# Layer 0's first products in three weight chunks and four accumulators, with x transposed between them

## The chip, the cores and the metric

The kernel runs on one core of a Trainium2 chip. The metric is the device time of one execution in microseconds (us), the median of several runs. The engines are TensorE (PE in the profile; its weight loads are PEld), VectorE (DVE), ScalarE (ACT), GpSimd (POOL) and SyncE (SP), which here issues the weight transfers.

## The reference, cut to what matters

Two post-norm transformer layers over 512 tokens of width 1024. Each layer attends to its own tokens and, with four heads, to a memory of 256 rows, and then runs a SwiGLU (a mixture of experts in layer 1). The change touches the first lines of layer 0: the memory's keys and values, and what stands right behind them.

```
kvm = mem @ w_mem_kv[i]                 # (256, 1024) @ (1024, 512)
km = kvm[..., :hm]; vm = kvm[..., hm:]  # hm = 256: keys, values
proj = x @ w_in_swa[j]                  # (512, 1024) @ (1024, 1408): q, k, v, qc
q, k = partial_rope(q, cos, sin), partial_rope(k, cos, sin)
```

## The kernel before, in words

Every product is made of three fp16 matmuls (`mm3`, lines 238 to 240): high by high, high by low and low by high. Weights arrive in f32 as chunks of at most 2096 columns per partition. Each chunk is loaded by one DMA on SP's queue (line 123) into one of three `raw` buffers. ACT then writes its high part (`wh<-raw`, line 150) and DVE its low part (`wl<-raw`, line 159), in pieces of `W.piece` columns, 1048 unless it is set otherwise. `W.tick(n)` puts n such steps into the program where it is called: one new ACT piece, and one DVE piece of those that are waiting, as long as more than `LAG = 1` wait. `W.need(i)` forces all pieces up to chunk i; a use of a weight calls it. A fourth load can only be issued when the first chunk has been converted.

The order on each engine is the order in which the program is written; nothing is moved later. At the start (lines 699 to 761) this order is:

1. SP loads the memory's 256 rows (two DMAs), the two chunks of `w_mem_kv[0]`, the four tiles of x, and then, as buffers come free, `w_in_swa`.
2. PE transposes the memory (line 742). ACT and DVE copy it out as `memTh` and `memTl`.
3. Four steps follow: keys of heads 0 and 1, keys of heads 2 and 3, values of the first 128 rows, values of the last 128. Each is 24 matmuls over all of K in one PSUM bank of 256 columns (8 blocks of 128 rows of K, three matmuls each). Behind each step stand its copies out of PSUM (`k_evac` is four ACT and two DVE instructions, a value tile one and one), then `W.tick(2)`, which converts a chunk of `w_in_swa`, then the 8 transposes of one tile of x (`transposed`, line 391) with two ACT and two DVE copies, `xTh` and `xTl`.
4. DVE works out the angles of the rotary embedding from the positions (lines 752 to 760, 24 small instructions), ACT the sine and cosine.
5. `v_proj(t)` for the four tiles of x: 24 matmuls of 192 columns each, with the first unit of `w_in_swa` (`u_a`, two chunks of 4 blocks of K, 448 columns a block, converted in pieces of 1048 and 744 columns). The query projections and the attention of layer 0 follow.

PSUM has four single banks (`bank()`) and two tiles of two banks (`bank2()`), each group used in turn.

Of the kernel before, what the change touches and what calls it, by code (L numbers as in the profile page):

```python
# [19 lines left out]
NT = S // 128  # L20
KD = D // 128
# [5 lines left out]
ML = 256  # L27
# [17 lines left out]
SQ = 8.0  # L45
SV = 8.0
SP = 4096.0
SG = 32768.0
DS = 1.0 / (SX * SW)
# [3 lines left out]
PIECE = 1048  # L53
# [157 lines left out]
def trunk_kernel(ctx, tc, x, mem, positions, w_in_swa, attn_sinks, w_in_fox, b_forget, w_mem_kv, w_out,  # L211
# [13 lines left out]
    def bank(name="A"):  # L225
        return ps.tile([128, 512], FT, name="bk", tag="A", bufs=4)

    def bank2():
        return ps.tile([128, 2, 512], FT, name="bk2", tag="S", bufs=2)

    def high(o, i, scale=1.0):
        nc.scalar.activation(o, i, AF.Copy, scale=scale)  # L232

    def low(o, i, scale, h):
        nc.vector.scalar_tensor_tensor(o, i, scale, h, op0=OP.mult, op1=OP.subtract)  # L235

    def mm3(o, lh, ll, rh, rl, first, last, **kw):
        nc.tensor.matmul(o, lh, rh, start=first, stop=False, **kw)  # L238
        nc.tensor.matmul(o, lh, rl, start=False, stop=False, **kw)  # L239
        nc.tensor.matmul(o, ll, rh, start=False, stop=last, **kw)  # L240
# [5 lines left out]
    W = Weights(nc, rawp, hlp)  # L246

    def wsrc(w):
        return w.rearrange("(k p) c -> p k c", p=128)

    def add_cols(w, c0, c1):
        v = wsrc(w)
        return W.add((v[:, 0:4, c0:c1], 4 * (c1 - c0)), (v[:, 4:8, c0:c1], 4 * (c1 - c0)))
# [11 lines left out]
    def unit(u, n):  # L265
        return [View(W, u, i, n) for i in range(2)]

    u_m0 = add_cols(w_mem_kv[0], 0, 512)
    u_a = add_cols(w_in_swa[0], 960, 1408)
    u_k = add_cols(w_in_swa[0], 512, 960)  # L270
    u_q = add_cols(w_in_swa[0], 0, 512)
# [56 lines left out]
    xtok = base.tile([128, NT, D], FT, name="xtok")  # L328
    xT = (xTp.tile([128, KD, S], FH, name="xTh"), xTp.tile([128, KD, S], FH, name="xTl"))
    memT = (memp.tile([128, KD, ML], FH, name="memTh"), memp.tile([128, KD, ML], FH, name="memTl"))  # L330
# [54 lines left out]
    def transposed(src, dst, t, before=lambda q: None):  # L385
        for q in range(2):
            before(q)
            b = bank()
            bv = b.rearrange("p (k n) -> p k n", n=128)
            for k in range(4):  # L390
                nc.tensor.transpose(bv[:, k, :], src[:, (4 * q + k) * 128:(4 * q + k + 1) * 128], identf)
            o = (slice(None), slice(4 * q, 4 * q + 4), slice(t * 128, (t + 1) * 128))
            high(dst[0][o], bv, SX)
            low(dst[1][o], bv, SX, dst[0][o])

    def halves(half):
        return slice(64 * half, 64 * half + 64), slice(64 - 64 * half, 128 - 64 * half)
# [13 lines left out]
    def k_evac(KH, KL, heads, src, sc, cols):  # L411

        for half in range(2):
            for r in halves(half):
                high(KH[r, heads(half), cols], src(half), sc)
        for half in range(2):
            a = halves(half)[0]
            low(KL[a], src(half), sc, KH[a, heads(half), cols])
# [199 lines left out]
    def mem_kv(u, memT, KM, VM):  # L618
        def kpair(p):
            wh, wl = unit(u, 512)  # L620
            b = bank()[:, :ML]
            c = slice(p * 128, p * 128 + 128)
            for k in range(KD):
                mm3(b, wh[:, k, c], wl[:, k, c], memT[0][:, k, :], memT[1][:, k, :], k == 0, k == KD - 1)
            k_evac(KM[0], KM[1][:, p, :], lambda hf: 2 * p + hf, lambda hf: b[64 * hf:64 * hf + 64, :], DS * SQ,
                   slice(0, ML))

        def vtile(m):
            wh, wl = unit(u, 512)
            b = bank()[:, :ML]  # L630
            c = slice(m * 128, m * 128 + 128)
            for k in range(KD):
                mm3(b, memT[0][:, k, c], memT[1][:, k, c], wh[:, k, 256:], wl[:, k, 256:], k == 0, k == KD - 1)
            high(VM[0][:, m, :], b, DS * SV)
            low(VM[1][:, m, :], b, DS * SV, VM[0][:, m, :])
            if m == 1:
                W.free(u)

        return [lambda: kpair(0), lambda: kpair(1), lambda: vtile(0), lambda: vtile(1)]
# [55 lines left out]
    def mem_tiles(pool):  # L695
        return ((pool.tile([128, MH, ML], FH, name="KMh"), pool.tile([128, MH // 2, ML], FH, name="KMl")),
                (pool.tile([128, 2, ML], FH, name="VMh"), pool.tile([128, 2, ML], FH, name="VMl")))

    KM0, VM0 = mem_tiles(sp)
    memtok = [sp.tile([128, D], FT, name="P", bufs=3) for _ in range(2)]  # L700
    mr = mem[0].rearrange("(t p) d -> p t d", p=128)
    for t in range(2):
        nc.sync.dma_start(memtok[t], mr[:, t, :])
    W.load_n(2)
    for t in range(NT):
        nc.sync.dma_start(xtok[:, t, :], xr[:, t, :])
    W.load()
# [30 lines left out]
    for t in range(2):  # L738
        for q in range(2):
            b = bank().rearrange("p (k n) -> p k n", n=128)  # L740
# [2 lines left out]
            o = (slice(None), slice(4 * q, 4 * q + 4), slice(t * 128, (t + 1) * 128))  # L743
            high(memT[0][o], b, SX)
            low(memT[1][o], b, SX, memT[0][o])
    m0 = mem_kv(u_m0, memT, KM0, VM0)
    for i, f in enumerate(m0):
        f()
        W.tick(2)
        transposed(xtok[:, i, :], xT, i)  # L750

    nc.vector.tensor_copy(posf, pos)
    for j in range(8):
# [155 lines left out]
    for i, u in enumerate(u_fi):  # L909
        wh, wl = unit(u, 256)  # L910
        if i == 0:
            bb = [bank2(), bank2()]
            for t in range(NT):
                if t == NT - 1:
                    transposed(xtok[:, t, :], xT, t)
                c = slice(t * 128, t * 128 + 128)
                for jj in range(2):
                    f = slice(jj * 128, jj * 128 + 128)
# [7 lines left out]
        else:  # L926
            for jj in range(2):
                f = slice(jj * 128, jj * 128 + 128)
                b = bank2()
# [18 lines left out]
    for h in range(2):  # L948
# [6 lines left out]
        for gi, u in enumerate(u_fo[h]):  # L955
            kn = (8, 8, 6)[gi]
            wh, wl = unit(u, 512)
            for t in range(NT):
                c = slice(t * 128, t * 128 + 128)
# [29 lines left out]
    wh, wl = unit(u_xv2, 524)  # L989
    for t in range(NT):  # L990
        c = slice(t * 128, t * 128 + 128)
        b = bank()
# [294 lines left out]
    def fetch(pool, oh, n, rows_too=True):  # L1287

        b = bank()
        idx = pool.tile([128, 2], I32, name="idx", bufs=2)  # L1290
        to = pool.tile([128, 2], I32, name="to", bufs=2)
        rows = []
        for r, m in n:
            i = r // 128
            for t in range(NT):
                nc.tensor.matmul(b[:m, 2 * i:2 * i + 2], oh[:, t, r:r + m], tid[:, t, :], start=t == 0,
                                 stop=t == NT - 1)
        for r, m in n:
            i = r // 128
            if not rows_too:  # L1300
                break
            nc.vector.tensor_copy(idx[:m, i:i + 1], b[:m, 2 * i:2 * i + 1])
            g = pool.tile([128, D], FT, name=f"xg{i}")
            nc.gpsimd.indirect_dma_start(out=g[:m, :], out_offset=None, in_=x2d,
                                         in_offset=bass.IndirectOffsetOnAxis(ap=idx[:m, i:i + 1], axis=0))
            rows.append(g)
        sums_at(pool, b, n, to)
        return rows, b, idx, to
# [262 lines left out]
    with tc.For_i(0, nit) as _:  # L1571
# [35 lines left out]
        rows, b, _, to = fetch(lp, oh, n)  # L1607
# [153 lines left out]
    for s in range(NEXP):  # L1761
        C = CAP[s]
        act = [mx.tile([128, KF, CMAX], FH, name=f"act{i}", bufs=1) for i in range(2)]
        for i, u in enumerate(u_ei[s]):
            if i < 2 * QUADS:
                if i % 2 == 0:
                    sa = mx.tile([128, 4, CMAX], FT, name="sa", bufs=2)
                b = bank2()
# [82 lines left out]
```

## Time and profile before

| | |
|---|---|
| median of 3 runs | 1679.88 us (1676.76 to 1680.16) |
| the profiled execution: its own time | 1677.88 us |
| its span in the profile | 1676.1 us |
| PE busy | 1616.5 us, 96% |
| DVE busy | 1225.9 us, 73% |
| ACT busy | 981.9 us, 59% |
| mean granted clock of TensorE | 0.984 |

The span is the time from the first to the last instruction of the profiled execution; 1.78 us lie around it. Matmuls are pipelined, so a busy PE is not a PE at its peak: the step from the start of one matmul to the start of the next tells how fast they run.

### The profile page before, as it was taken

How to read it: one execution, taken by the hardware profiler on the slowest of the kernel's cores; microseconds unless marked ns; L12 is line 12 of the kernel's file. 1: busy time of each engine (PE TensorE's matmuls, PEld its weight loads, DVE VectorE, ACT ScalarE, POOL GpSimd, SP SyncE). 2: the span in 40 equal slices, each digit the busy share in tenths (PEclk: the TensorE clock that was granted, in tenths of full speed). 3: DMA queues.
4: the chain of work that ended last, by engine and by line, in shares of the span. 5: the costliest groups of instructions: out<-in, count | busy, mean ns of one | idle time of the engine just before them, and what ended most of it. 6: DMA issues, size and time to landing. Idle time of an engine off the chain costs nothing.

```text
span 1676.1 us, 42682 instructions
## 1 busy us (share of the span) xinstructions
PE 1616.5 (96%) x18407; PEld 1278.2 (76%) x18407; DVE 1225.9 (73%) x1814; ACT 981.9 (59%) x1507; POOL 283.7 (17%) x280
## 2 busy tenths in 40 slices
PE   7999999999999799999799999999999999999996
PEld 6775564444444647665599999999999999999993
DVE  6788644333532658787799698996979979699997
ACT  5676333322212457665287687776877778665773
POOL 0342200000100400003130031201303031130250
PEclk8999999999999899999899999999999999999998
DMA  7511033322632132110499899999999999999993
GB/s 264 177 52 51 1 126 126 100 101 88 206 100 69 61 126 84 33 61 16 170 378 326 308 376 393 370 340 318 384 367 365 365 321 371 343 287 371 351 369 117
DMA packets 180531, 370.13 MB, mean 221 GB/s; under 512 B 6573, under 2 KB 49581, under 8 KB 180336
## 3 DMA queue, kind: packets, MB, share of 16 engines
q1 hardware_dynamic: 173264, 343.48, 57.4%
q0 software_dynamic: 4768, 15.47, 3.9%
q10 hardware_dynamic: 2304, 8.39, 1.3%
q8 instruction: 146, 2.39, 0.6%
q14 instruction: 49, 0.40, 0.1%
HBM read 355.08 MB, written 12.39 MB: 219 GB/s over the span
## 4 chain that ended last, share of the span: by engine, by line
PE 39%; issue 3%; DVE 3%; ACT 2%; DMA 2%; POOL 2%; ACTq 0%; POOLq 0%; DVEq 0%
PE bk L1387 8%; PE bk L1389 8%; PE bk L1388 8%; PE bk L1416 4%; PE bk L1417 4%; PE bk L1418 4%; DVE wl L159 2%; ACT wh L150 1%; DMA raw<-in_w_exp_in_dram 1%; POOL act L1405 1%; PE bk L238 1%; PE bk L239 1%; PE bk L240 1%; POOL expert_sums L1320 1%; PE bk L1437 1%
## 5 line engine op out<-in xcount | busy, mean ns | idle before, releaser
L159 DVE SCALAR_TENSOR_TENSOR wl<-raw,wh 128x1048 f16<-128x1048 f32 (+3 forms) x654 | 794.4, 1265 | 104.4 <-ACT wh L150 104.1
L150 ACT ACTIVATE wh<-raw 128x1048 f16<-128x1048 f32 (+3 forms) x654 | 641.1, 1041 | 102.5 <-PE bk L240 49.6
L1387 PE MATMUL bk<-xa,wh 128*128 128x160 f16 (+3 forms) x1280 | 261.3, 232 | 5.7 <-DVE eid L1538 5.7
L1388 PE MATMUL bk<-xa,wh 128*128 128x160 f16 (+3 forms) x1280 | 261.2, 232 | 0.0
L1389 PE MATMUL bk<-xa,wl 128*128 128x160 f16 (+3 forms) x1280 | 261.1, 232 | 0.0
L1387 PEld LDWEIGHTS <-wh 128*128 128x128 f16 x2560 | 250.8, 98 | 6.5 <-issue 5.8
L1388 PEld LDWEIGHTS <-wh 128*128 128x128 f16 x2560 | 250.8, 98 | 2.7 <-issue 2.4
L1389 PEld LDWEIGHTS <-wl 128*128 128x128 f16 x2560 | 250.8, 98 | 0.0
L1418 PE MATMUL bk<-act,wl 128*128 128x160 f16 (+6 forms) x1232 | 235.3, 227 | 1.4 <-DVE wl L159 1.4
L1417 PE MATMUL bk<-act,wh 128*128 128x160 f16 (+6 forms) x1232 | 235.3, 227 | 0.0
L1416 PE MATMUL bk<-act,wh 128*128 128x160 f16 (+6 forms) x1232 | 235.3, 227 | 0.0
L1387 PE MATMUL bk<-xe,wh 128*128 128x128 f16 (+2 forms) x1280 | 223.2, 221 | 2.1 <-DVE sa L1403 1.4
L1388 PE MATMUL bk<-xe,wh 128*128 128x128 f16 (+2 forms) x1280 | 223.1, 221 | 0.0
L1389 PE MATMUL bk<-xe,wl 128*128 128x128 f16 (+2 forms) x1280 | 223.1, 221 | 0.0
L238 PE MATMUL bk<-xTh,wh 128*128 128x512 f16 (+2 forms) x656 | 205.7, 324 | 4.9 <-DVE KLx L235 4.0
L239 PE MATMUL bk<-xTl,wh 128*128 128x512 f16 (+2 forms) x656 | 205.5, 323 | 0.5 <-DVE xTl L235 0.5
L240 PE MATMUL bk<-xTh,wl 128*128 128x512 f16 (+2 forms) x656 | 205.5, 323 | 0.0
L1405 POOL TENSOR_TENSOR act<-sa,act 128x512 f16<-128x512 f32 (+6 forms) x40 | 106.8, 2671 | 280.7 <-ACT act L232 280.7
L238 PEld LDWEIGHTS <-wh 128*128 128x128 f16 x944 | 92.8, 98 | 55.3 <-DVE KLx L235 4.4
L240 PEld LDWEIGHTS <-wl 128*128 128x128 f16 x944 | 92.8, 98 | 48.6 <-DVE wl L159 1.6
L239 PEld LDWEIGHTS <-wh 128*128 128x128 f16 x944 | 92.9, 98 | 47.3 <-issue 1.6
L1418 PEld LDWEIGHTS <-wl 128*128 128x128 f16 x1232 | 120.5, 98 | 1.8 <-DVE wl L159 1.8
(349 smaller groups left out, 2787.4 us busy)
## 6 DMA issues: line engine op xcount, KB each, us to landing
raw<-in_w_exp_in_dram SPq DMA_DIRECT2D x176, 1024.0 KB, 9.0
raw<-in_w_exp_out_dram SPq DMA_DIRECT2D x85, 1024.0 KB, 9.3
raw<-in_w_ffn_in_dram SPq DMA_DIRECT2D x22, 1024.0 KB, 5.2
raw<-in_w_out_dram SPq DMA_DIRECT2D x8, 1024.0 KB, 5.0
raw<-in_w_ffn_out_dram SPq DMA_DIRECT2D x8, 1024.0 KB, 5.6
raw<-in_w_in_fox_dram SPq DMA_DIRECT2D x8, 1024.0 KB, 5.2
raw<-in_w_mem_kv_dram SPq DMA_DIRECT2D x4, 1024.0 KB, 7.1
raw<-in_w_in_swa_dram SPq DMA_DIRECT2D x4, 896.0 KB, 8.9
```

The lines of the kernel that those rows point to most:

```text
L150: self.nc.scalar.activation(h[:, p:e], t[:, p:e], AF.Copy, scale=SW)
L159: self.nc.vector.scalar_tensor_tensor(l, src, SW, h, op0=OP.mult, op1=OP.subtract)
L238: nc.tensor.matmul(o, lh, rh, start=first, stop=False, **kw)
L239: nc.tensor.matmul(o, lh, rl, start=False, stop=False, **kw)
L240: nc.tensor.matmul(o, ll, rh, start=False, stop=last, **kw)
L1387: nc.tensor.matmul(o, wh[:, k, c], xe[0][:, k, :C], start=first, stop=False, skip_group_check=True)
L1388: nc.tensor.matmul(o, wh[:, k, c], xe[1][:, k, :C], start=False, stop=False, skip_group_check=True)
L1389: nc.tensor.matmul(o, wl[:, k, c], xe[0][:, k, :C], start=False, stop=k == KD - 1, skip_group_check=True)
L1405: lambda: nc.gpsimd.tensor_sub(act[1][:, j, :C], sa[:, :, :C], act[0][:, j, :C])]
L1416: nc.tensor.matmul(o, wh[:, k, c], act[0][:, kk, :C], start=first, stop=False, skip_group_check=True)
L1417: nc.tensor.matmul(o, wh[:, k, c], act[1][:, kk, :C], start=False, stop=False, skip_group_check=True)
L1418: nc.tensor.matmul(o, wl[:, k, c], act[0][:, kk, :C], start=False, stop=kk == KF - 1, skip_group_check=True)
```

## The change

`w_mem_kv[0]` becomes three chunks of 2, 2 and 4 blocks of K in place of two of 4 and 4. All three are loaded ahead of x, which takes all three `raw` buffers. While they are converted, `W.piece` is 512. The four results (keys of two head pairs, values of two tiles) get an accumulator each, in two tiles of two banks, `kb` and `vb`. Chunk one is multiplied into all four, then chunk two, then comes the first tile of x to transpose, and then chunk three, one result at a time, each followed by its copies and the next tile of x. The conversions of `w_in_swa` that stood between the steps now stand behind all of them, as `W.tick(4)`.

```
--- before.py
+++ after.py
@@ -265,7 +265,8 @@
     def unit(u, n):
         return [View(W, u, i, n) for i in range(2)]
 
-    u_m0 = add_cols(w_mem_kv[0], 0, 512)
+    wm = wsrc(w_mem_kv[0])
+    u_m0 = W.add(*[(wm[:, a:b, :], 512 * (b - a)) for a, b in ((0, 2), (2, 4), (4, 8))])
     u_a = add_cols(w_in_swa[0], 960, 1408)
     u_k = add_cols(w_in_swa[0], 512, 960)
     u_q = add_cols(w_in_swa[0], 0, 512)
@@ -701,7 +702,7 @@
     mr = mem[0].rearrange("(t p) d -> p t d", p=128)
     for t in range(2):
         nc.sync.dma_start(memtok[t], mr[:, t, :])
-    W.load_n(2)
+    W.load_n(3)
     for t in range(NT):
         nc.sync.dma_start(xtok[:, t, :], xr[:, t, :])
     W.load()
@@ -743,11 +744,39 @@
             o = (slice(None), slice(4 * q, 4 * q + 4), slice(t * 128, (t + 1) * 128))
             high(memT[0][o], b, SX)
             low(memT[1][o], b, SX, memT[0][o])
-    m0 = mem_kv(u_m0, memT, KM0, VM0)
-    for i, f in enumerate(m0):
-        f()
-        W.tick(2)
-        transposed(xtok[:, i, :], xT, i)
+    W.piece = 512
+    kb, vb = bank2(), bank2()
+
+    def m0_part(u, ks, ps_):
+
+        wh, wl = unit(u, 512)
+        for p in ps_:
+            for k in ks:
+                if p < 2:
+                    c = slice(p * 128, p * 128 + 128)
+                    mm3(kb[:, p, :ML], wh[:, k, c], wl[:, k, c], memT[0][:, k, :], memT[1][:, k, :], k == 0, k == KD - 1)
+                else:
+                    c = slice((p - 2) * 128, (p - 2) * 128 + 128)
+                    mm3(vb[:, p - 2, :ML], memT[0][:, k, c], memT[1][:, k, c], wh[:, k, 256:], wl[:, k, 256:],
+                        k == 0, k == KD - 1)
+
+    for ks in ((0, 1), (2, 3)):
+        m0_part(u_m0, ks, range(4))
+    W.need(W.first[u_m0 + 1] - 1)
+    transposed(xtok[:, 0, :], xT, 0)
+    for p in range(4):
+        m0_part(u_m0, range(4, KD), [p])
+        if p < 2:
+            k_evac(KM0[0], KM0[1][:, p, :], lambda hf, p=p: 2 * p + hf, lambda hf, p=p: kb[64 * hf:64 * hf + 64, p, :ML],
+                   DS * SQ, slice(0, ML))
+        else:
+            high(VM0[0][:, p - 2, :], vb[:, p - 2, :ML], DS * SV)
+            low(VM0[1][:, p - 2, :], vb[:, p - 2, :ML], DS * SV, VM0[0][:, p - 2, :])
+        if p < NT - 1:
+            transposed(xtok[:, p + 1, :], xT, p + 1)
+    W.free(u_m0)
+    W.piece = PIECE
+    W.tick(4)
 
     nc.vector.tensor_copy(posf, pos)
     for j in range(8):
```

The first place where instructions move is DVE's queue around the angles. `xTl` are the copies of x, `KMl` and `VMl` those of keys and values, line 159 is a piece of weights, and the rows from `posf` (a cast) to the last `n_132` are the angles. Before, the queue goes:

```order
L159 SCALAR_TENSOR_TENSOR wl<-raw,wh 128x744
L159 SCALAR_TENSOR_TENSOR wl<-raw,wh 128x1048
L235 SCALAR_TENSOR_TENSOR xTl<-bk,xTh 128x4x128 x2
L235 SCALAR_TENSOR_TENSOR VMl<-bk,VMh 128x256
L159 SCALAR_TENSOR_TENSOR wl<-raw,wh 128x744
L159 SCALAR_TENSOR_TENSOR wl<-raw,wh 128x1048
L235 SCALAR_TENSOR_TENSOR xTl<-bk,xTh 128x4x128 x2
L752 CAST posf<-pos 128x4
```

Of the change, the same queue up to the angles, and then the end of the angles:

```order
L235 SCALAR_TENSOR_TENSOR xTl<-bk,xTh 128x4x128 x2
L235 SCALAR_TENSOR_TENSOR VMl<-bk,VMh 128x256
L235 SCALAR_TENSOR_TENSOR xTl<-bk,xTh 128x4x128 x2
L235 SCALAR_TENSOR_TENSOR VMl<-bk_168,VMh 128x256
L159 SCALAR_TENSOR_TENSOR wl<-raw,wh 128x1048
L159 SCALAR_TENSOR_TENSOR wl<-raw,wh 128x744
L159 SCALAR_TENSOR_TENSOR wl<-raw,wh 128x1048
L781 CAST posf<-pos 128x4
```

```order
L730 SCALAR_TENSOR_TENSOR ang<-n_132,ang 128x32 x3
L786 TENSOR_SCALAR ang<-ang 128x32
L788 SCALAR_TENSOR_TENSOR n_132<-ang 128x32
L789 TENSOR_SCALAR n_132<-n_132 128x32
L159 SCALAR_TENSOR_TENSOR wl<-raw,wh 128x744
L235 SCALAR_TENSOR_TENSOR Vl<-bk,Vh 128x192 x2
```

Before, the pieces of `u_a` stand among the copies, and the one behind the angles belongs to the unit after `u_a`. Now three pieces of `u_a` stand behind all copies, and its fourth, the last 744 columns, stands behind the angles.

The second place is ACT's queue: the copies of the last tiles of x and of the values, and then the pieces of `u_a` (line 150). Before:

```order
L232 ACTIVATE VMh<-bk 128x256
L150 ACTIVATE wh<-raw 128x1048
L150 ACTIVATE wh<-raw 128x744
L232 ACTIVATE xTh<-bk 128x4x128 x2
L232 ACTIVATE VMh<-bk 128x256
L150 ACTIVATE wh<-raw 128x1048
L150 ACTIVATE wh<-raw 128x744
L232 ACTIVATE xTh<-bk 128x4x128 x2
L758 ACT_TABLE_LOAD
```

Of the change:

```order
L232 ACTIVATE VMh<-bk_168 128x256
L232 ACTIVATE xTh<-bk 128x4x128 x2
L232 ACTIVATE VMh<-bk_168 128x256
L150 ACTIVATE wh<-raw 128x1048
L150 ACTIVATE wh<-raw 128x744
L150 ACTIVATE wh<-raw 128x1048
L150 ACTIVATE wh<-raw 128x744
L787 ACT_TABLE_LOAD
```

The pieces shown of before are those of the unit behind `u_a`; the pieces of `u_a` stood between the copies of the keys. In the change all four pieces of `u_a` stand behind the last copy.

The third place is PE's queue between the first result and the second, with the semaphores that rows wait for. Before, behind the first 24 matmuls stand the transposes of x's first tile and then the second keys, in a bank of their own:

```order
L391 MATMUL bk<-identf,xtok 128x128 [waits DMAHW4_49,PE_49]
L391 MATMUL bk<-identf,xtok 128x128 x3
L391 MATMUL bk<-identf,xtok 128x128 [waits PE_49]
L391 MATMUL bk<-identf,xtok 128x128 x3
L238 LDWEIGHTS wh
L238 MATMUL bk<-memTh,wh 128x256 [waits PE_49]
```

Of the change, behind the first result (`bk_167` is `kb`) the transposes of x's second tile and the second keys:

```order
L392 MATMUL bk<-identf,xtok 128x128 [waits DMAHW6_49,PE_49]
L392 MATMUL bk<-identf,xtok 128x128 x3
L392 MATMUL bk<-identf,xtok 128x128 [waits PE_49]
L392 MATMUL bk<-identf,xtok 128x128 x3
L238 LDWEIGHTS wh
L238 MATMUL bk_167<-memTh,wh 128x256 [waits DVE_49]
```

The second keys go into the tile that DVE is still copying the first keys out of, and their first matmul waits for DVE. The second values wait in the same way for DVE's copy of the first, in `vb`.

## Rows read from the trace of the kernel before

**Rows 1.** The page's head.

```profile
span 1676.1 us, 42682 instructions
```

**Rows 2.** Waits of PE, whole run: total us, times, longest.

```profile
PE bk L238 <- DVE KMl L235: 8.8, 1, 8.8
...
PE bk L238 <- ACT wh L150: 3.7, 1, 3.7
...
PE bk L391 <- DVE xTl L235: 2.1, 1, 2.1
```

**Rows 3.** Stretches: length, busy us (instructions) by engine, granted clock, DMA.

```profile
11.40:17.40 6.00, 5.24 (x24) 3.06 (x25) 4.72 (x4) 2.96 (x4) 0.00 (x0) 0.50 1.03 406
24.20:27.60 3.40, 3.40 (x19) 2.30 (x18) 2.73 (x5) 3.36 (x6) 0.00 (x0) 0.53 0.05 17
41.00:860.00 819.00, 789.97 (x5928) 474.57 (x5926) 491.64 (x1016) 378.49 (x782) 115.40 (x196) 0.98 0.30 100
```

**Rows 4.** Timeline of PE: start us, length, instruction, count [idle before].

```profile
17.35 0.38 PE L240 MATMUL bk<-memTh,wl 128*128 128x256 f16 x1
...
29.53 0.27 PE L238 MATMUL bk<-wh,memTh 128*128 128x256 f16 x1
...
32.04 0.27 PE L240 MATMUL bk<-wh,memTl 128*128 128x256 f16 x1
32.15 1.04 PE L391 MATMUL bk<-identf,xtok 128*128 128x128 f32 x8
33.02 0.25 PE L238 MATMUL bk<-wh,xTh 128*128 128x192 f16 x1
...
34.92 0.25 PE L240 MATMUL bk<-wh,xTl 128*128 128x192 f16 x1
...
40.86 0.25 PE L240 MATMUL bk<-wh,xTl 128*128 128x192 f16 x1
```

**Rows 5.** Timeline of ACT, the same columns.

```profile
10.35 2.00 ACT L150 ACTIVATE wh<-raw 128x1048 f16<-128x1048 f32 x2 [1.89 <-DMA raw<-in_w_mem_kv_dram]
13.05 2.00 ACT L150 ACTIVATE wh<-raw 128x1048 f16<-128x1048 f32 x2 [0.69 <-DMA raw<-in_w_mem_kv_dram]
17.77 1.54 ACT L232 ACTIVATE KMh<-bk 64x256 f16<-64x256 f32 x4 [2.72 <-PE bk L240]
20.60 1.79 ACT L150 ACTIVATE wh<-raw 128x1048 f16<-128x1048 f32 x2 [1.28 <-DMA raw<-in_w_in_swa_dram]
...
28.86 0.38 ACT L232 ACTIVATE VMh<-bk 128x256 f16<-128x256 f32 x1 [1.14 <-PE bk L240]
29.14 1.78 ACT L150 ACTIVATE wh<-raw 128x1048 f16<-128x1048 f32 x2
```

**Rows 6.** Timeline of DVE, the same columns.

```profile
19.35 0.86 DVE L235 SCALAR_TENSOR_TENSOR KMl<-bk,KMh 64x256 f16<-64x256 f32 x2 [2.83 <-ACT KMh L232]
...
25.84 2.10 DVE L159 SCALAR_TENSOR_TENSOR wl<-raw,wh 128x744 f16<-128x744 f32 x2
27.97 1.29 DVE L235 SCALAR_TENSOR_TENSOR xTl<-bk,xTh 128x512 f16<-128x512 f32 x2
29.27 0.42 DVE L235 SCALAR_TENSOR_TENSOR VMl<-bk,VMh 128x256 f16<-128x256 f32 x1
...
36.34 0.16 DVE L752 CAST posf<-pos 128x4 f32<-128x4 int32 x1
...
40.34 0.18 DVE L760 TENSOR_SCALAR n<-n 128x32 f32<-128x32 f32 x1
```

**Rows 7.** Conversions in the first 110 us by shape: count, busy us, mean ns, idle.

```profile
L159 DVE SCALAR_TENSOR_TENSOR wl<-raw,wh 128x1048 f16<-128x1048 f32 x13 | 16.2, 1245 | 7.4 <-ACT wh L150 7.4
L150 ACT ACTIVATE wh<-raw 128x1048 f16<-128x1048 f32 x13 | 14.0, 1076 | 3.9 <-DMA raw<-in_w_mem_kv_dram 2.6 <-DMA raw<-in_w_in_swa_dram 1.3
...
L159 DVE SCALAR_TENSOR_TENSOR wl<-raw,wh 128x744 f16<-128x744 f32 x4 | 3.7, 926 | 0.0
...
L150 ACT ACTIVATE wh<-raw 128x744 f16<-128x744 f32 x4 | 3.2, 811 | 0.0
```

## The prediction

> **What bounds the kernel now.** I read the page's head first for the span [rows 1], then PE's waits [rows 2]. After the first 25 us only one wait is long (8.8 us, at the end of layer 0's FFN); from 41 to 860 us PE is busy 790 of 819 us, DVE 492 and ACT 378 [rows 3]. So PE's queue, in its written order, is the bound there, and a product that starts late at the beginning makes all that follows late by as much. Then I read the beginning on three timelines: PE [rows 4], ACT [rows 5], DVE [rows 6]. PE waits 3.7 us for the first converted piece and 2.1 us for a bank that DVE must empty [rows 2], and after each wait its products run at half clock for 6.0 and 3.4 us [rows 3]. That is what there is to win. From 33.02 on, where `v_proj` starts, PE runs without a gap to the last product of `v_proj(3)` at 40.86 [rows 4]. I compare the two kernels at that product and carry the difference to the end.
>
> **What is earlier.** The two chunks of the memory's weights land at 10.35 and 13.05 [rows 5], so a chunk takes 2.7 us, and half a chunk should land at about 9.0. A piece of 512 columns costs, along the straight line through the shapes of 744 and 1048 [rows 7], some 0.61 us on ACT and 0.68 on DVE, of which the next starts 0.07 before the end. The third matmul of the first block of K can then start at 9.0 + 0.61 + 0.04 + 0.68 = 10.3, the second block at 10.9. A full-speed step between products of 256 columns is (32.04 - 29.53) / 23 = 0.109 us [rows 4], at half clock 0.22, so the first chunk's 24 products last to about 15.3. The first half-clock stretch covered 6.0 us from the first product on; the first product is now at 9.7, and I let the clock rise at 15.7. The remaining products take 22 x 0.109 = 2.4 us (to 18.1), the transposes of x's first tile 33.02 - 32.15 = 0.87 [rows 4], and the 12 products that finish the first keys 1.3. These end at T0 = 20.3.
>
> T0 has bounds from both sides. It can't be before 16.5, because the third chunk still lands at 13.05 and its four pieces need 0.61 + 0.04 + 0.68 + 3 x 0.61 on ACT and DVE (16.2), the last products 0.3 more. If the clock stayed at half all along, it would be 15.3 + 24 x 0.22 + 0.9 + 12 x 0.22 = 24.
>
> The load of `u_a` now waits until a chunk is converted, but its bytes stand behind x's in the queue as before, and its first half was there at 20.6 [rows 5]. Nobody asks for it before 26, so that costs nothing; a load late by all of that reserve would start to cost.
>
> **What is later, first part: the shared accumulators.** From T0 the first product of the second keys waits for DVE's copy of the first. ACT starts 17.77 - 17.35 - 0.38 = 0.04 us after the last product and needs 1.54 [rows 4, 5]; DVE follows after 0.04 and needs 0.86 [rows 6]. So the second keys start at T0 + 2.5, with the 0.87 of transposes inside, and end at T0 + 3.8. Then the same copies again (T0 + 6.3), behind them DVE's two copies of x's third tile (1.29, T0 + 7.5) and the copy of the first values (0.42, T0 + 7.9) [rows 6], for which the second values wait. Those end at T3 = T0 + 7.95 + 1.3 = T0 + 9.2 = 29.5. Before, the same point is 32.04 + 0.27, or 32.3 [rows 4]. Here the change is ahead by almost 3 us.
>
> **What is later, second part: the pieces of `u_a`.** Before, they were converted among the copies and `v_proj` found them ready. Now ACT and DVE begin them at T3. ACT: 0.04, then 0.28 until the value copy gives way (28.86 to 29.14) and 1.07 for the piece [rows 5, 7], so `v_proj(0)` starts at T3 + 1.4. DVE: the first low piece 1.25 less overlap (T3 + 2.6), then a pair of 744 and 1048 columns in 2.10 [rows 6], to T3 + 4.65. Now the queue of DVE goes into the angles: from 36.34 to 40.34 + 0.18 they took 4.18 us [rows 6]. Only then comes the fourth piece, 0.93 us [rows 7], done at T3 + 9.75. `v_proj(0)` needs it for its last two blocks of K (the seventh block straddles columns 896 to 1088 of the chunk, the pieces meet at 1048). Its second matmul of that block waits there, all of PE behind it. Before, the piece that stood behind the angles belonged to the next unit, and nobody waited for it.
>
> Five products are left, at half clock 0.165 each ((34.92 - 33.02) / 23 = 0.083 at full speed [rows 4]), since PE has been idle for over 4 us, twice the gap after which it fell before [rows 2, 3]. The last product of `v_proj(0)` starts at T3 + 9.8 + 0.65 = T3 + 10.4 = 39.9. Before it was at 34.92 [rows 4]: 5.0 us late.
>
> Then 72 products to the end of `v_proj(3)`. Half-clock stretches after an idle PE were 3.4 and 6.0 us [rows 3]; less the 0.65 already counted, half of it is lost: 1.4 to 2.7, I take 2.0.
>
> **The sum.** -3 at T3 (inside the times above), +5.0 at the last product of `v_proj(0)`, +2.0 of clock: 7.0 us late at the last product of `v_proj(3)`. The four pieces of the next unit move from ahead of `v_proj` to between its steps, some 4 us of ACT and DVE; PE's busy 790 of 819 us against their 378 and 492 covers them [rows 3], and without that cover the unit's last piece would cost up to 1.25 us. The four pieces more per engine that 512 columns make cost 0.1 to 0.2 us each, all inside T0. The profiled execution took 1677.88 us (span 1676.1 [rows 1] and 1.78 around it), so 1684.9 by it, 1686.9 by the median of the three runs, which is 2.0 higher. I say 1686. What a measurement of this kernel can tell from no change is about 0.2%, 3.4 us.
>
> **A rule weighed against the rows.** The first half-clock stretch began after an idle 3.7 us and ended 6.0 us after the first product [rows 2, 3]; from that one execution I took 15.7 for the rise. The Trainium skill, TensorE: Matmul & The Clock Gate, Part 1, says that the number of slow products at a start varies between runs of one kernel. By it 15.7 isn't a constant: T0 would lie anywhere between the bounds above and the sum with it, from 3 to 11 us, instead of 7.0. The trace has one execution, so no row here shows it.
>
> **The rivals.**
>
> *The clock falls again between T0 and T3* (chance 0.20). PE has gaps there of about 1.6 us (T0 + 0.9 to + 2.5) and 1.0, and a gap of 2.1 was enough before [rows 2]. Two of the groups of 12 products lie on the chain, each 1.3 longer at half clock: +2.6, so 9.6 us late, about 1688.5. Against it: each gap is shorter than the one that did it. The Trainium skill, the same page, Part 4, says that transposes don't count as PE-busy in the way that products do. By it this rival would be the likelier, as a good part of PE's work there is transposes; the trace doesn't show it, since the transposes at 32.15 stand between dense products.
>
> *The clock stays high from the first product on* (0.12). The idle ahead of it shrinks from 3.7 to about 1.9 us, as the first product moves from about 11.5 to 9.7. Then T0 is at its bound of 16.5, 3.8 earlier, and the sum is 7.0 - 3.8 = 3.2 us, about 1682, at the edge of no change. Against it: the products of the first chunks wait for pieces again and again, and 2.1 us of idle were enough for a fall.
>
> *The delay is taken up later* (0.08). PE's wait of 8.8 us [rows 2] would swallow 7 if it ended at a fixed time. It ends on DVE's copy of `KMl` of layer 1, which waits for the last tokens' norm and so for PE; that moves along. Then about 1680.
>
> *Faster* (0.04). From 41 to 860 us the granted clock is 0.98 [rows 3]: some 33 us at half level, 16 us of loss. If the shift against the clock's decisions made over 10 us of that loss disappear, the kernel would come out 3.5 us faster, about 1676. It decides from two thirds of that loss on; I see no reason that so much should go one way.
>
> **How the numbers follow.** Forecast as worked out, 3.4 to 9 us late: 0.56, its own range 1682 to 1689. With the first rival slower has 0.76; the clock held high and the delay taken up are no change, 0.20; faster 0.04. The range for 8 in 10 leaves out the faster case and half of no change below, and of the slower cases those with T0 near 24: 1680.5 to 1690.5.
>
> **What would show it.** Right: first product before 10.5; PE idle 1 to 2 us ahead of the second keys and about 1 ahead of the second values, both released by DVE; `v_proj(0)`'s last blocks waiting some 4 to 5 us on a DVE piece (line 159), with the angles ahead of it on DVE; half clock behind that; the last product of `v_proj(3)` near 48 and not 40.86. Wrong: `v_proj(0)` running through, or that product late and the end not. The number would be wrong if the clock rose at another point than 15.7, by up to 4 us either way.

## The result and the profile after

The change takes 1687.98 us (median of 5 runs, 1686.76 to 1689.85) against 1679.88 (1676.76 to 1681.21) before: a ratio of 1.0052, 95% interval 1.0037 to 1.0066. It is slower, by some 8 us. The forecast was 1686.0 in a range of 1680.5 to 1690.5, with a chance of 0.76 on slower. The execution shown here is the slowest of the five, 1689.85 us, so its distance to the profiled execution of before, 12 us, is more than the kernel's.

PE's waits in the first 110 us of the change (total us, times, longest) answer to [rows 2]:

```profile
PE bk L239 <- DVE wl L159: 5.8, 4, 4.0
...
PE bk L238 <- ACT wh L150: 2.7, 2, 1.4
PE bk L238 <- DVE KMl L235: 1.7, 1, 1.7
PE bk L238 <- DVE VMl L235: 1.1, 1, 1.1
```

The wait of 3.7 us for the first piece has shrunk and that of 2.1 for a bank is gone. In their place stand 1.7 and 1.1 us for the shared accumulators, 1.4 for the first piece of `u_a`, and 5.8 for its low pieces, 4.0 of it for the last. PE's timeline shows them in order (start us, length, instruction [idle before]; compare [rows 4]):

```profile
9.65 0.28 PE L238 MATMUL bk<-memTh,wh 128*128 128x256 f16 x1 [1.30 <-ACT wh L150]
...
17.75 0.27 PE L240 MATMUL bk<-memTh,wl 128*128 128x256 f16 x1
17.86 1.04 PE L392 MATMUL bk<-identf,xtok 128*128 128x128 f32 x8
20.55 0.27 PE L238 MATMUL bk<-memTh,wh 128*128 128x256 f16 x1 [1.65 <-DVE KMl L235]
...
26.20 0.27 PE L238 MATMUL bk<-wh,memTh 128*128 128x256 f16 x1 [1.12 <-DVE VMl L235]
...
27.40 0.27 PE L240 MATMUL bk<-wh,memTl 128*128 128x256 f16 x1
29.11 0.24 PE L238 MATMUL bk<-wh,xTh 128*128 128x192 f16 x1 [1.44 <-ACT wh L150]
...
32.39 0.24 PE L239 MATMUL bk<-wl,xTh 128*128 128x192 f16 x1 [0.50 <-DVE wl L159]
...
32.93 0.37 PE L238 MATMUL bk<-wh,xTh 128*128 128x192 f16 x1
37.33 0.32 PE L239 MATMUL bk<-wl,xTh 128*128 128x192 f16 x1 [4.03 <-DVE wl L159]
...
37.92 0.36 PE L240 MATMUL bk<-wh,xTl 128*128 128x192 f16 x1
...
46.28 0.25 PE L240 MATMUL bk<-wh,xTl 128*128 128x192 f16 x1
46.36 0.38 PE L238 MATMUL bk<-xTh,wh 128*128 128x512 f16 x1
```

The first keys end at 17.75 + 0.27 = 18.0 (the forecast's T0), the second values at 27.7 (T3), 4.6 us ahead of before's 32.3. `v_proj` even starts 3.9 us earlier (29.11 against 33.02). Then it stops on its seventh block, and its last product stands at 46.28 instead of 40.86: 5.4 us late. DVE's timeline shows what the stop waited for:

```profile
29.09 3.25 DVE L159 SCALAR_TENSOR_TENSOR wl<-raw,wh 128x1048 f16<-128x1048 f32 x3 [0.54 <-ACT wh L150]
32.26 0.16 DVE L781 CAST posf<-pos 128x4 f32<-128x4 int32 x1
...
36.26 0.18 DVE L789 TENSOR_SCALAR n<-n 128x32 f32<-128x32 f32 x1
36.35 0.93 DVE L159 SCALAR_TENSOR_TENSOR wl<-raw,wh 128x744 f16<-128x744 f32 x1
```

Three low pieces, the whole angles, then the fourth low piece, done at 37.28; PE goes on 0.05 us later. The stretches (columns as in [rows 3]: length, then PE, PEld, DVE, ACT and POOL busy, granted clock, DMA) show the clock:

```profile
9.60:18.00 8.40, 7.92 (x70) 6.75 (x71) 6.16 (x11) 4.94 (x9) 0.00 (x0) 1.00 1.04 407
...
32.00:33.00 1.00, 0.61 (x6) 0.59 (x6) 0.97 (x10) 0.74 (x1) 0.00 (x0) 0.83 0.58 50
33.00:36.90 3.90, 0.29 (x2) 0.08 (x1) 3.38 (x18) 0.46 (x2) 0.00 (x0) 0.50 0.59 225
36.90:43.00 6.10, 5.67 (x37) 5.22 (x37) 1.21 (x4) 2.13 (x4) 0.00 (x0) 0.51 0.53 172
43.00:48.00 5.00, 5.00 (x51) 4.14 (x49) 3.31 (x5) 2.54 (x5) 0.00 (x0) 1.00 0.12 18
```

It was at its full level (2.4 GHz) from the first product on, as the lengths of 0.27 us say too. It fell to half (1.2 GHz) at about 32.6, ahead of the long wait and not in it: the product at 32.39 still takes 0.24 us, the one at 32.93, the last before the wait, 0.37. What PE did before the fall were few products between the waits of 1.44, 1.04, 0.19 and 0.50 us for the first pieces of `u_a`. The clock stayed at half through the wait, and for 5.5 us after it the products ran at half.

The delay then grows. The scores of layer 0's attention on the first keys, in before and in the change (duration min/median/max, first and last start):

```profile
L497 PE MATMUL bk<-KMh,Q x16: 272/283/284, 56.4 to 79.9; 128*128 128x256 f16 x16
```

```profile
L498 PE MATMUL bk<-KMh,Q x16: 272/283/283, 61.3 to 87.1; 128*128 128x256 f16 x16
```

The first is 4.9 us late, the last 7.2: 23.5 us from first to last have become 25.8. From there to the last score on the layer's own keys (162.1 before, 169.7 after) little is added. ACT's timeline of the change at the start of this stretch:

```profile
58.14 2.00 ACT L150 ACTIVATE wh<-raw 128x1048 f16<-128x1048 f32 x2
60.99 2.00 ACT L150 ACTIVATE wh<-raw 128x1048 f16<-128x1048 f32 x2 [0.85 <-DMA raw<-in_w_out_dram]
63.02 0.49 ACT L820 ACTIVATE qk<-bk 128x384 f32<-128x384 f32 x1
```

The second pair of pieces is one that before did not convert here. The copy of the keys (`qk`) stands behind it. Between 46 and 95 us PE now waits four times behind copies, 1.6 us in all (before once, 0.2); the rest of the 2.3 us does not stand in these waits:

```profile
PE bk L842 <- POOL qk L833: 0.6, 1, 0.6
PE bk L551 <- ACT qk L820: 0.4, 1, 0.4
PE bk L238 <- ACT qk L820: 0.4, 1, 0.4
PE bk L238 <- DVE PTl L235: 0.2, 1, 0.2
```

### The profile page after: what moved, and what is told of

It reads as the page before. It is cut to its first block, busy times and chain, and to the rows that moved or that the text cites. A ratio compares the mean times of both kernels' runs of the same rounds, so it can differ in the third digit from the quotient of the medians.

```text
span 1688.1 us, 42696 instructions
## 1 busy us (share of the span) xinstructions
PE 1620.3 (96%) x18407; PEld 1280.8 (76%) x18407; DVE 1226.5 (73%) x1818; ACT 983.0 (58%) x1511; POOL 283.9 (17%) x280
## 4 chain that ended last, share of the span: by engine, by line
PE 39%; issue 3%; DVE 3%; DMA 2%; ACT 2%; POOL 2%; ACTq 0%; POOLq 0%; DVEq 0%
PE bk L1416 8%; PE bk L1418 8%; PE bk L1417 8%; PE bk L1445 4%; PE bk L1447 4%; PE bk L1446 4%; DVE wl L159 2%; DMA raw<-in_w_exp_in_dram 1%; ACT wh L150 1%; POOL act L1434 1%; PE bk L238 1%; PE bk L240 1%; PE bk L239 1%; POOL expert_sums L1349 1%; PE bk L1466 1%
```

## The experiments

The theory after this profile: the change loses 5 us because `u_a`'s last piece stands behind the angles, with the half clock that follows, and 2 us because four pieces of the next unit are late for the attention; the three chunks and the order of the products cost nothing. The rivals: the new order of products, the shared accumulators or the small pieces cost by themselves. Ten kernels ran, against before on the same chip (medians 1678.65, 1678.31 and 1678.05 in three groups).

**e1_need: all of `u_a` ahead of the angles.**

```
-    W.tick(4)
+    W.need(W.first[u_a + 1] - 1)
```

> All four pieces of u_a are converted ahead of the angles; nothing else differs from the change. Theory (the fourth piece behind the angles on DVE, and the half clock that follows, make most of the loss): PE's wait of 4.0 us in v_proj(0) goes, its last product starts near 34 and that of v_proj(3) near 40 to 42 in place of 46.3; the loss of some 2 us in the attention stays, since the next unit's pieces still stand late. About 1682 us, 5 to 6 below the change. Rival (the waits for the shared accumulators, 1.7 and 1.1 us, make the loss): no gain beyond 1 us, about 1687.

Measured: 1681.02 us, ratio 1.0018 (1.0009 to 1.0027). The loss falls from 8.1 us to 2.4 (against its own before). PE's waits in the first 110 us show that the wait of 4.0 is gone:

```profile
PE bk L238 <- ACT wh L150: 2.7, 2, 1.4
PE bk L239 <- DVE wl L159: 1.7, 3, 1.0
PE bk L238 <- DVE KMl L235: 1.7, 1, 1.7
PE bk L238 <- DVE VMl L235: 1.1, 1, 1.1
```

The half clock did not all go with it. It began at 32.3 us, behind the same short waits and with no long wait near, and 22 products ran at half (38 in the change). PE's timeline, from its first slow product to its last:

```profile
32.26 0.32 PE L240 MATMUL bk<-wh,xTl 128*128 128x192 f16 x1
...
35.58 0.31 PE L240 MATMUL bk<-wh,xTl 128*128 128x192 f16 x1
```

The first query product starts at 40.7, ahead of before's 41.45. What is left stands in the attention, which still takes 25.9 us from the first to the last of these scores:

```profile
L498 PE MATMUL bk<-KMh,Q x16: 273/283/283, 55.6 to 81.5; 128*128 128x256 f16 x16
```

**e2_between: the pieces of x's weights between the steps again**, as before had them, with all else of the change.

```
     W.need(W.first[u_m0 + 1] - 1)
+    W.piece = PIECE
...
+        W.tick(2)
         if p < NT - 1:
             transposed(xtok[:, p + 1, :], xT, p + 1)
     W.free(u_m0)
-    W.piece = PIECE
-    W.tick(4)
```

> The conversions of the next two units go back between the four results, as before the change; chunks and accumulators stay as in the change. Theory: v_proj finds u_a ready, the attention's loss of 2 us goes too, and the time comes down to that of the kernel before or a little lower, 1678 to 1682; ACT now waits for u_a's arrival (20.6 us) in front of x's second tile, so little of the earlier start is left. Rival (chunks of 512 columns and shared accumulators cost by themselves): above 1684.

Measured: 1677.44 us, ratio 0.9997 (0.9988 to 1.0006). The whole loss is gone; the attention takes 23.5 us (55.3 to 78.8). What the change wins at the front goes into waits for the shared accumulators, where DVE now has pieces to convert between the copies (PE's waits, the same stretch):

```profile
PE bk L238 <- DVE VMl L235: 3.5, 1, 3.5
PE bk L238 <- DVE KMl L235: 1.7, 1, 1.7
```

**e3_crossed: e2_between with keys and values that follow each other in different tiles.**

```
-    kb, vb = bank2(), bank2()
+    b2s = bank2(), bank2()
+    acc0 = [b2s[p % 2][:, p // 2, :ML] for p in range(4)]
...
```

> As the run before (conversions between the results), and each tile of two banks now holds one key and one value result, so that the second keys no longer wait for DVE's copy of the first. Theory: PE's waits for KMl and VMl of 1.7 and 1.1 us shrink, and v_proj starts 1 to 3 us earlier than in the run before: 1676 to 1680. Rival (ACT and DVE bound this stretch, the PE waits are only their shadow): the same as the run before within 1 us.

Measured: 1678.68 us, ratio 1.0001 (0.9992 to 1.0010). `v_proj` starts at 28.5 instead of 31.2. Part of that is the clock at the start, which was at its full level here and at half for 17 products in e2_between (here it fell later, from 25.9 to 29.9 us); e6_best below has the same accumulators and 17 slow products at the start, and starts at 29.5, so about 1.7 us are the accumulators'. But the gain is gone one step later, as PE's timeline shows:

```profile
39.96 0.59 PE L238 MATMUL bk<-xTh,wh 128*128 128x512 f16 x1 [3.04 <-DVE Vl L235]
```

The first query product needs the bank of the first values of x, whose copy `Vl` stands behind the angles on DVE (39.55). And the products behind this wait ran at half clock for 3.4 us.

**e4_warm: the change with 48 products that nobody reads, in the idle of `v_proj(0)`.**

```
+            if t == 0 and k == 6:
+                for _ in range(48):
+                    nc.tensor.matmul(kb[:, 0, :192], xT[0][:, 0, c], wh[:, 0, :192], start=True, stop=True)
...
```

> The change, with 48 products more on PE ahead of the seventh block of K in v_proj(0); their result is never read. They fill the 4.0 us in which PE waits for the fourth piece. Theory: the clock stays at its full level behind the wait, the 5.4 us of half-clock products at 37.3 to 42.7 run at full, 2.7 us are saved, and the wait itself stays: about 1685.3. Rival (the wait alone costs, half clock is hidden by the copies of v): 1688, no gain.

Measured: 1686.92 us, ratio 1.0056 (1.0042 to 1.0070). `v_proj` starts 1.4 us later than in the change (30.5, the clock was at half near 11.5 in this execution), its first query product 1.1 earlier (45.2): 2.5 us less in between, near the expected 2.7. The clock fell here too (at 31.8 us), but the added products ran through the wait, and from about 35 us on it was at its full level. In the ratio to before nothing of this shows: each of the two intervals reaches some 2.3 us to either side, so the times neither show a saving of 2.7 us nor exclude it. The clock's share of the loss is read from the front of one execution alone.

**e5_lead: e1_need and half of the next unit's pieces ahead of the angles.** One line, `W.tick(2)`, behind `W.need`.

> The kernel of e1_need (every conversion of u_a's x pieces ahead of the angles), and behind it the first chunk of the next unit (u_k) is converted there too, ahead of the angles. Theory: the 2.3 us that the change loses inside layer 0's first attention comes from the pair of ScalarE conversions of u_k that it makes in that attention's second step; so the stretch from the first query product to the last score on the first keys falls from 40.8 us to about 38.4, and the time to about 1679, 2 us under e1_need. Rival: the loss there has another cause; the stretch stays at 40.8 and the time at 1681.

Measured: 1682.46 us, ratio 1.0025 (1.0016 to 1.0035): not faster, and the attention got longer, 29.6 us. The theory as put there failed. On ACT the extra pair in the second step is gone; another, ahead of the first copy of keys, is still there and later than in e1_need. ACT's timeline and PE's waits:

```profile
52.31 4.37 ACTq L426 DMA_DIRECT2D lng<-in_ln_attn_g_dram  x1
...
57.96 2.00 ACT L150 ACTIVATE wh<-raw 128x1048 f16<-128x1048 f32 x2 [2.84 <-issue]
59.99 0.49 ACT L821 ACTIVATE qk<-bk 128x384 f32<-128x384 f32 x1
```

```profile
PE bk L843 <- POOL qk L834: 3.1, 1, 3.1
```

Issuing one DMA from ACT (the load of `lng`) took 4.37 us here (0.38 in the change), ACT's queue stood behind it, PE waited 3.1 us for the keys, and from 62.3 us on, in that wait, the clock was at half for 6.8 us. What made the issue slow is open: in e9_all, which converts still earlier, the same issue took 0.38.

**e9_all: e5_lead with all four pieces there** (`W.tick(4)`), so that ACT has the order of before from the first query product on.

> The kernel of e5_lead with all four pieces of the next unit that before converts ahead of the angles converted there (e5_lead had two of them); from the first query product on, ScalarE's order of copies and conversions is then that of before. Theory: the change's loss inside the first attention is the price of those four pieces being late, wherever on ScalarE they fall; with all four back, the stretch from the first query product to the last score on the first keys is 38.4 us as before (40.8 in e1_need, 44.6 in e5_lead), and the time 1678 to 1681, as the angles come later. Rival: the loss comes from the change's order itself; the stretch stays over 40 and the time at 1681 or more.

Measured: 1682.58 us, ratio 1.0029 (1.0018 to 1.0041). The attention is whole again, 23.5 us from the first to the last score on the first keys:

```profile
L498 PE MATMUL bk<-KMh,Q x16: 273/283/283, 61.7 to 85.2; 128*128 128x256 f16 x16
```

The stretch that the expectation named, from the first query product at 45.1, is 40.1, because the clock fell at its start (0.57 from 45 to 49 us), which is outside the attention. The time isn't better, since these pieces have to wait for their own load ahead of the angles (ACT's timeline):

```profile
37.69 1.79 ACT L150 ACTIVATE wh<-raw 128x1048 f16<-128x1048 f32 x2 [2.82 <-DMA raw<-in_w_in_swa_dram]
...
43.72 0.23 ACT L788 ACTIVATE sin<-ang 128x32 f32<-128x32 f32 x1 [2.95 <-DVE ang L787]
```

The angles end 3.6 us later than before's, and PE waits 3.4 for `Vl` behind them. So the four late pieces are the cause of the attention's loss, since the rest of the change's order is kept here; put ahead of the angles they cost at least as much there.

**e7_chunks: before with the three chunks and the small pieces alone**, in the old order with banks of their own.

```
-    u_m0 = add_cols(w_mem_kv[0], 0, 512)
+    wm = wsrc(w_mem_kv[0])
+    u_m0 = W.add(*[(wm[:, a:b, :], 512 * (b - a)) for a, b in ((0, 2), (2, 4), (4, 8))])
...
-    W.load_n(2)
+    W.load_n(3)
...
+    W.piece = 512
...
+        W.piece = PIECE
         W.tick(2)
```

> The kernel before with one part of the change alone: the memory's weights are loaded in three chunks and converted in pieces of 512 columns; keys, then values, then x's transposes in the old order, with banks of their own. Theory: the chunks start the first product about 2 us earlier, and little of it is left at the end of the first values of x, which wait for conversions of x's own weights: 1677 to 1680. Rival: chunks and smaller pieces cost by themselves, and carry the change's loss: over 1682.

Measured: 1678.55 us, ratio 1.0000 (0.9992 to 1.0009). The first product starts at 9.74 instead of 11.48, `v_proj` at 33.1 as before (33.02). The chunks and small pieces cost nothing and bring nothing that the interval, 1.4 us to either side, can show.

**e8_angles: before with the block of the angles behind `v_proj`**, and **e6_best: e3_crossed with the same move**. The edit moves the lines from `nc.vector.tensor_copy(posf, pos)` to the cosine:

```
     for t in range(NT):
         v_proj(t)
         W.tick(1)
+    nc.vector.tensor_copy(posf, pos)
...
+    nc.scalar.activation(cos, n1, AF.Sin)
     qc_proj(*unit(u_a, 448), 192, Qm)
```

> The kernel before with the block of the angles alone moved behind the products of the first values of x, as in e6_best; its control. Theory: in the order of before nothing on TensorE waits long for VectorE's copies there (0.34 us), so the time stays at 1678 to 1679.5. Rival: the angles cost in before as well, and the time falls by 2 us or more without any of the change.

> The kernel of e3_crossed (pieces of x between the products, crossed accumulators), with the block of the angles (positions to cosine) moved behind the products of the first values of x. Theory: what gave back e3_crossed's early start was the 3.0 us wait for VectorE's copy of the first of those values, which stands behind the angles; without it the first query product starts near 37 us (39.96 in e3_crossed, 41.45 before) and the time is 1674 to 1675, about 4 us below before. Rival: the sine and cosine are then late for the rotation of the queries, or VectorE is late elsewhere, and the gain is taken up: 1678, as e3_crossed.

Measured: e8_angles 1676.49 us, ratio 0.9988 (0.9979 to 0.9997), 1.5 us under the range of the theory: the rival's 2 us are nearly reached. The wait of 0.34 us for `Vl` is gone and the first query product starts 1.05 earlier; the rest can't be placed. e6_best 1677.85, ratio 0.9997 (0.9988 to 1.0006). There the first query product starts at 37.6, 3.8 us ahead of before, near what was expected (37), but ACT then stands still, as its timeline shows:

```profile
47.04 0.23 ACT L801 ACTIVATE sin<-ang 128x32 f32<-128x32 f32 x1 [3.01 <-DVE ang L800]
...
47.61 1.18 ACT L232 ACTIVATE Q<-bk 64x512 f16<-64x512 f32 x2
```

The queries' copies come behind the sine, and the attention takes 25.7 us instead of 23.5. This is the rival's first half, and its time.

**e10_mid: e6_best with the angles behind the second of the four `v_proj`.**

```
         W.tick(1)
+        if t == 1:
+            nc.vector.tensor_copy(posf, pos)
...
```

> The kernel of e6_best with the block of the angles in the middle of the products of the first values of x, behind the second of four. Theory: in e6_best the queries' copies on ScalarE stood behind the sine, which waited 3.0 us for the angles, and the first attention gave back 2.1 of the 3.8 us gained; with the angles some 4 us earlier the stretch from the first query product to the last score on the first keys is 38.4 instead of 40.6 and the time 1675 to 1676. Rival: the angles then hold VectorE's copies of the last two values, the first query product starts 2 us later, and the time stays at 1677 to 1678.

Measured: 1674.90 us, ratio 0.9978 (0.9969 to 0.9987). The sine is at 42.6, the first query product at 37.1, the last score on the first keys at 76.1 (79.9 before). The scores again:

```profile
L498 PE MATMUL bk<-KMh,Q x16: 272/283/283, 52.1 to 76.1; 128*128 128x256 f16 x16
```

This version beats both kernels: 3.1 us under before, and by the two ratios some 12 under the change (0.74% of 1680). How much of the 3.1 is owed to the chunks and accumulators stays open: e8_angles has 1.8 us without them, the two intervals meet, and before with the angles in the middle was not run.

| | `v_proj` starts | first query product | attention, first to last score | last own-key score | median us | ratio to before |
|---|---|---|---|---|---|---|
| before | 33.0 | 41.45 | 23.5 | 162.1 | 1679.88 | |
| the change | 29.1 | 46.4 | 25.8 | 169.7 | 1687.98 | 1.0052 |
| e1_need | 28.9 | 40.7 | 25.9 | 162.4 | 1681.02 | 1.0018 |
| e2_between | 31.2 | 40.4 | 23.5 | 161.4 | 1677.44 | 0.9997 |
| e3_crossed | 28.5 | 40.0 | 23.5 | 162.4 | 1678.68 | 1.0001 |
| e4_warm | 30.5 | 45.2 | 25.8 | 168.6 | 1686.92 | 1.0056 |
| e5_lead | 30.6 | 41.3 | 29.6 | 168.6 | 1682.46 | 1.0025 |
| e9_all | 30.9 | 45.1 | 23.5 | 166.1 | 1682.58 | 1.0029 |
| e7_chunks | 33.1 | 41.5 | 23.5 | 160.9 | 1678.55 | 1.0000 |
| e8_angles | 32.5 | 40.4 | 23.5 | 161.3 | 1676.49 | 0.9988 |
| e6_best | 29.5 | 37.6 | 25.7 | 159.2 | 1677.85 | 0.9997 |
| e10_mid | 29.0 | 37.1 | 24.0 | 160.0 | 1674.90 | 0.9978 |

Landmarks are from one execution each, medians from 5 to 12. The median of before itself lay between 1678.05 and 1679.88 in the groups, so kernels are compared by their ratios.

## Why the prediction was right, step by step

**First product.** Forecast 9.7, measured 9.65; the third matmul 10.3 and 10.37. Right.

**The clock at the start, T0.** Forecast 20.3, measured 18.0. The clock did not fall, as the second rival (0.12) had it. That rival's T0 of 16.5 was too early: it counts the pieces and leaves out PE's own time, which from 9.7 on is at least 60 products at the full-speed step and the transposes, 9.7 + 60 x 0.109 + 0.87 = 17.1. So a clock that stays high was worth 2.3 us here and not 3.8, and the rival's sum would have been 4.7. The high clock is no constant of this code. In the nine kernels that begin like the change, the first 24 products all ran at full speed in three executions (the change, e1_need, e3_crossed) and 14 to 17 of them at half in the other six; in five of these the clock fell at about 11.2 us, behind 5 to 10 products at full, and in e10_mid the first products are the slow ones. In before, e7_chunks and e8_angles 23 or all 24 of them were slow. The Trainium skill, TensorE: Matmul & The Clock Gate, Part 1, says that the number of slow products varies between runs; these executions, of different kernels with the same instructions there, agree, and the term was -2.3 us in this one.

**The shared accumulators.** Second keys at T0 + 2.5: measured 20.55, T0 + 2.5. T3 = T0 + 9.2: measured T0 + 9.7. Right; e6_best against e2_between shows the price of shared tiles where pieces stand between the copies: `v_proj` at 29.5 instead of 31.2. The first rival, a fall of the clock between T0 and T3, did not come about in the change, nor in the four executions of e1_need, e4_warm, e5_lead and e9_all, which have the same order there. The Trainium skill, the same page, Part 4, says that transposes don't count as PE-busy in the way of products; the forecast took a fall for likelier by it, and between T0 and T3 these five do not show one. The reason that was given against this rival, gaps shorter than the 2.1 us of before, doesn't carry either: in e3_crossed the clock fell at 25.9 behind gaps of 1.23 and 0.82 us, and in e2_between it stayed up behind one of 3.45. The length of a gap alone does not tell.

**`u_a`'s fourth piece behind the angles.** Forecast 4 to 5 us of wait, the piece done at T3 + 9.75; measured 4.03 and T3 + 9.6. e1_need confirms it: 5.7 of the 8.1 us go away with that order alone, 4.0 as the wait and about 1.2 as half clock (16 slow products fewer, 0.16 us apart instead of 0.083). The last product of `v_proj(0)` is 37.92 against 34.92, 3.0 late instead of 5.0: the T0 term again.

**The half clock behind it.** Forecast 2.0 in the 72 products that follow; measured (46.28 - 37.92) - (40.86 - 34.92) = 2.4. The size was right, the reason was not: the forecast put it down to an idle of over 4 us, but the clock had fallen at 32.6, ahead of the wait. e1_need, without that wait, had the fall at 32.3, and e4_warm, e5_lead and e9_all at 31.8 to 31.9. These five are the kernels in which PE waits for the first pieces of `u_a` behind T3; in the others the clock does not fall at that place. So the fall goes with those short waits, and against e1_need the long one added 16 of the 38 slow products. So 5.4 us late at the last product of `v_proj(3)`, where 7.0 was forecast.

**The pieces of the next unit.** This step failed. It said that PE's busy 790 us against ACT's 378 cover them, and that without this cover the last piece would cost up to 1.25 us. They cost 2.3 us, not at the end of the unit but in the attention, where they stand ahead of copies that PE waits for. A cover read from 819 us says nothing of a stretch in which ACT's queue is what releases PE. e9_all (all four pieces early, 23.5 us) and e2_between (in their old places, 23.5) against e1_need (25.9) show that their lateness is the cause.

**The sum.** 5.4, less 0.5 (before waited 0.34 us ahead of its first query product, and now nothing does), plus 2.3, is 7.2 at the last score on the first keys; 7.6 at the last own-key score; 8.1 in the medians. So the number was right by two misses that nearly cancel: the start cost 1.6 less than forecast, the attention 2.3 more. What stays open is the last half microsecond, and why the profiled execution lost 4 us more after 620 us: it had 3.4 us of half clock from 743 us on and 13.7 from 834 on, before 10.2 near 820 to 837 in two parts. The two others that are 6 us late by then, e4_warm and e5_lead, had the same 3.4 and 13.7; whether the lateness brings them was not tested.

**The delay is not taken up later, and there was no gain in the clock**: the third rival and the fourth, the faster one, are out. PE's wait of 8.8 us stands in the change as it did before (PE's waits of the whole run; the other 1.7 are the second keys'):

```profile
PE bk L238 <- DVE KMl L235: 10.4, 2, 8.8
```

The forecast calls it the only long one behind the first 25 us. That was misread: before has others of 5.7 and 3.6 us behind 760 us. They stand in the change too, at 5.5 and 3.6.

## What to carry to other kernels

Work that is put in program order ahead of a wait is as dear as the first thing that needs it: four pieces of weights cost nothing between the steps, 5 us when their last stood behind a block that nobody was waiting for yet, and the four behind them 2 us more. Before an order is changed, write down for each engine the queue from the moved instruction to the next one that another engine waits for, and check the cover there and not over the whole kernel. And an earlier start is worth something only when every following queue is free: here 4 us at `v_proj` were worth nothing at the end until the pieces were back in their places, the accumulators crossed and the angles moved. That version is 3 us under before, and moving the angles alone gives 1.8 of these. Last, look for what the clock did before a wait and not only behind it: here it had fallen already.

## What the runs showed of the hardware

A DMA issue on ACT that took 0.38 us in the change took 4.37 us in e5_lead and 2.18 in e6_best; the cause is open. Gaps of PE and falls of the clock do not go together by length alone: it fell behind 2.12 us (before) and behind 1.23 and 0.82 (e3_crossed), and stayed up behind 3.45 (e2_between). The second keys waited 1.65 us for the copies of the first, which lie in the other bank of the same tile, and did not when the two lay in different tiles (e3_crossed and e6_best, 0.8 us left at a later result). That wait is one that the program's semaphores ask for, for a tile as a whole; whether the banks would need it no run shows. In e10_mid, e7_chunks and e8_angles the view of stretches gives a granted clock of 1.00 over the first products (in e10_mid from 9.60 to 18.00), while most of these are 0.39 to 0.42 us long and step at half speed: at the very start the lengths of the products are the better witness.
